# Depthwise convolution of five of eight channel blocks: from scaled additions on VectorE to diagonal products on TensorE

## The chip, the cores and the metric

The kernel runs on one core of one Trainium2 chip. The metric is device time in microseconds, the median of several executions. Engines are named as the profile names them: PE (TensorE; PEld its weight loads), DVE (VectorE), ACT (ScalarE), POOL (GpSimd), SP (SyncE, which here only issues DMAs).

## The reference, cut to what matters

Two layers of a backbone over 256 latent and 256 context tokens with 1024 channels. The change concerns the first layer's mixer: one input projection feeds the heads of a state-space scan (SSD) and a conformer module; both go into one output projection, then a mixture of experts.

```python
def conformer_conv(v, gate, dw_w, dw_b, ln_g, ln_b, rows):
    u = v * jax.nn.sigmoid(gate)
    b, n, ch = u.shape
    if rows is not None:
        u = u.reshape(b * rows, GRID_W, ch)
    u = dwconv(u, dw_w, dw_b).reshape(b, n, ch)
    return jax.nn.silu(layernorm(u, ln_g, ln_b))
```

`dwconv` is a depthwise convolution along the tokens: 31 taps here, a weight for each tap and channel, zeros beyond the ends. The context is one sequence of 256 tokens; the latent tokens are four rows of 64, each convolved by itself.

## The kernel before, in words

Activations lie with 128 channels on the partitions and 512 tokens (256 context, 256 latent) on the columns. A **piece** is one block of 128 output columns of the input projection: 24 products of 128x128 weights with 512 columns (`cm_gemm`), in which weights and activations are split in high and low parts. Each piece needs its weights split first (`prep`, L465 on ACT, L466 on POOL), in one of two buffers. Weights come over SP's queue in 1 MB units into a ring of three tiles (`Stream`), in the order in which the program plans them.

The program is written in one order, and each engine keeps it. Work beside the products is written as generators: `step()` (L131) moves each one a step on, and `bg(us)` does so after a part of a piece and moreover takes entries from the list `bgq`, `RATE[0]` of them per microsecond of products (0.6, later 1.4). So what stands between two products in an engine's queue is set by these steps.

Four stretches follow each other, after a beginning of some 55 us:

- The SSD channels: 16 pieces, each followed by `conv5` (five taps on DVE, L772 and L774, then silu and transposes, L799). `CV_AT` puts three conformer blocks between them; a conformer block (`cvg_task`) is two pieces, value and gate.
- The SSD scan (`states`, `group`, `rest`: 16 groups of four heads) beside the list `FILL`: the two pieces each of the other five conformer blocks, and 16 modulation blocks (`mod_task`), each of two halves of four products with 32 weight columns in four column tiles (weights `sT`, moving columns from the ring).
- Eight pieces z that gate the SSD heads (`z_gate`, L1117 to L1129). What is left in `bgq` is written out behind them.
- The output projection, with the layer norm of the conformer channels beside its first half; then the experts and layer 1.

For each conformer block `cf_evac` writes the gated values into the tile `u`, rows with 15 zeros between them (602 columns), and puts 31 taps into `bgq`. A tap (L702, L704, L706) is one instruction on DVE over 572 columns: it adds `u`, shifted by the tap's place and scaled by that tap's weight of each channel, to one of two sums `ca`. The last one adds the two sums (L709, L710).

Of the kernel before, what the change touches and what calls it, by code (L numbers as in the profile page):

```python
# [27 lines left out]
class Stream:  # L28
    """Weights in the order of use, 2048 values a partition at a time, loaded ahead through rings of tiles."""
# [16 lines left out]
    def ring(self, tiles, last=None):  # L46
        """tiles [128, 2048] for the units up to the one of the key last"""
        self.rings.append((list(tiles), len(self.plan) if last is None else self.index[last] + 1))
        self.fill()

    def hold(self, held, fence=None):
        """no more loads for a while, for what must not wait behind them; fence: done on the next tile before its load"""
        self.held, self.fence = held, fence
        self.fill()

    def until(self, key=None, fence=None):
        """nothing after the unit of the key for now; fence: done on the next tile before its load"""
        self.limit = 1 << 30 if key is None else self.index[key] + 1
        self.fence = fence
        self.fill()  # L60
# [29 lines left out]
def build(tc, I, out):  # L90
# [32 lines left out]
    # ------------------------------------------------------------------ work beside the products  # L123
# [7 lines left out]
    def step(us=0.0, rate=0.0):  # L131
        """one step of everything that goes on beside the products, which took us since the last one"""
# [26 lines left out]
    class Slots:  # L159
        """tiles of rotating buffers, handed out when the last use of the buffer has been written down"""  # L160
# [17 lines left out]
        def take(self, *a):  # L178
            """for the work beside the products"""
            n = 0  # L180
            while (x := self.now(*a)) is None:
                n += 1
                assert n < 500
                yield
            return x

        def main(self, *a):
            """for the products"""
# [14 lines left out]
    # ------------------------------------------------------------------ the order of the weights  # L203
# [32 lines left out]
    CV_AT = {1: 0, 4: 1, 7: 2}  # L236
# [12 lines left out]
    for i in range(3, 8):  # L249
        for q in range(2):  # L250
            FILL.append(("cvg", i, q))
            for _ in range(2 if i < 7 else 0):
                FILL.append(MODS.pop(0))
    for f in FILL:
# [34 lines left out]
    # ------------------------------------------------------------------ constants  # L289
# [17 lines left out]
    def unit(pool, name, dt=F32):  # L307
        """8 KB of each partition; a later one of the same name takes the place of the first"""
# [68 lines left out]
    # 0 and 1 are exact in float32r  # L377
# [6 lines left out]
    # conditioning columns, silu, padded to 32 columns  # L384
# [23 lines left out]
    # ------------------------------------------------------------------ modulation  # L408
# [17 lines left out]
    def mod_block(l, b):  # L426
        """512 columns of the modulation of both conditionings, as columns [128, 4, 2]"""
# [19 lines left out]
    def row_bcast(dst, col):  # L447
        """dst [128, 1024] = the vector whose columns col(c) -> [128, 1], on every partition"""
# [12 lines left out]
    # ------------------------------------------------------------------ hi / lo parts of weights  # L461
    def prep(buf, w, eng=GP):
        """w [128, a, b] of 1024 values a partition -> its float32r high and low parts"""
# [5 lines left out]
    class Pieces:  # L469
        """the pieces of a list, prepared ahead in the free pairs of buffers"""  # L470
# [4 lines left out]
        def buffers(self, units, end=None):  # L475
            """for the pieces before the position end"""
# [13 lines left out]
        def release(self, n=None):  # L490
            """done with the n oldest pieces handed out"""
# [4 lines left out]
        def next(self, keep=False):  # L496
            """the next piece; the ones before it are done with, unless to be kept"""
# [63 lines left out]
    # ------------------------------------------------------------------ layer 0: norm, transposed input  # L561
    def quarter(u, i):
        """512 values of each partition of the tiles u"""
# [21 lines left out]
    def to_channels(p, k, gain, shift, hi, lo):  # L585
        """channel block k of the four token tiles, transposed -> modulated, split"""
# [21 lines left out]
    # the products over the first half of the input channels run before the second half is there  # L608
# [33 lines left out]
    stt.close()  # L642

    # ------------------------------------------------------------------ layer 0: input projection
# [15 lines left out]
    # layout of the padded conv input: 15 | ctx 256 | 15 | row 64 | 15 | row 64 | ... | 15  # L660
# [58 lines left out]

    def cm_task(sink):  # L720
        """one channel block; sink(accumulator) one step later"""
# [28 lines left out]
    def cvg_task(i):  # L750
        cm_task(lambda acc: PA.update(v=acc))
        cm_task(lambda acc: begin(cf_evac(i, PA.pop("v"), acc)))

    # SSD channels
# [59 lines left out]
    def lower_bounds():  # L814
        """of the forget gates: second row of the softmax over the layers"""
# [13 lines left out]
    def step_sizes(acc):  # L829
        """softplus, token-major [128, direction, tile, head]; decays"""  # L830
# [55 lines left out]
    begin(step_sizes(first[0]))  # L886
    for q in range(2):
        begin(conv5(8 + q, first[1 + q]))
    for i in range(8):
        for q in range(2 if i else 0):  # L890
            cm_task(lambda acc, j=2 * i + q: begin(conv5((8 + j) % 16, acc)))
        if i in CV_AT:
            cvg_task(CV_AT[i])
    drain()
    st1.close()

    # ------------------------------------------------------------------ layer 0: SSD beside the rest of the projection
# [17 lines left out]
    # high and low parts of the log decays  # L915
# [13 lines left out]
    def states():  # L929
        """carried states of both directions: decay * the one before + sum over the tile of B x dt decay-to-end"""  # L930
# [46 lines left out]
    def group(t, g):  # L977
        """the part of a tile's own tokens, for the four heads of a group"""
        b = []
        # log decays of the steps, of those up to each column  # L980
# [12 lines left out]
        # log decay from the row to the column, in whichever direction  # L993
# [27 lines left out]
        # channels of four heads on the partitions, tokens on the columns  # L1021
# [15 lines left out]
    def rest(t, hf):  # L1037
        """xs[t][hf] becomes the sum of the skip and state terms; added to the tile's own part"""
# [64 lines left out]
    # ------------------------------------------------------------------ layer 0: gate of the SSD heads  # L1103
# [57 lines left out]
    # ------------------------------------------------------------------ layer 0: output projection, conformer layer norm  # L1161
# [5 lines left out]
    # ------------------------------------------------------------------ router, fed while the output projections end  # L1167
# [12 lines left out]
    # the channels of the conformer, high and low  # L1180
# [6 lines left out]
    def router_pre(l, streams, pool):  # L1187
        """router weights times the gain of the norm, what its shift adds to the scores; both as rows"""
# [23 lines left out]
    def router_pair(X, streams, xg, pr, hf):  # L1212
        """512 columns of two tiles of X: squares of the norm, times the gain, transposed into the scores"""
# [59 lines left out]
    def moe_row(xg, t, i, c):  # L1273
        """a tile of rows for the experts; the columns from c on on ScalarE and GpSimd, those before on VectorE"""
# [20 lines left out]
    def ch_total(pq):  # L1295
        """sums of the four rows of each group, on every partition [128, 512]"""
# [10 lines left out]
    def layer_norm():  # L1307
        """beside the products of the first half of the output projection"""
# [66 lines left out]
    def tm_block(lhs, nt, sink, parts=1):  # L1375
        """512 output columns of nt token tiles; sink(t, accumulator) one step after the last product of each"""
# [62 lines left out]
    # ------------------------------------------------------------------ mixture of experts  # L1439
# [6 lines left out]
    # row of the result, row of the token, less BIG  # L1446
# [1279 lines left out]
```

## Time and profile before

| | |
|---|---|
| Device time, median of three runs | 1615.83 us (1612.98 to 1616.37) |
| Profiled execution, first to last instruction | 1616.7 us |
| PE busy, of the span | 1391.0 us (86%) |
| DVE busy | 1065.9 us (66%) |
| ACT busy | 748.6 us (46%) |
| POOL busy | 647.6 us (40%) |
| Taps (L706), count and busy time | 232, 258.4 us |
| HBM read, written | 321.44 MB, 9.44 MB |

Busy times are of one execution. Matmuls are pipelined, so their single durations overlap; the distance between starts is the better price. A mean duration in a group can hold several shapes. An fp32 product has two records. Idle time of an engine is put down to what ended it last.

### The profile page before, as it was taken

Reading aid. Unit: us, or ns where it says so; the run is one execution under the profiler, and the core shown is the slowest. Engines: PE = TensorE matmul, PEld = TensorE weight load, DVE = VectorE, ACT = ScalarE, POOL = GpSimd, SP = SyncE. Lnnn points to the kernel's source line nnn. Section 1 sums busy time; section 2 is a strip of 40 time slices with the busy share of each in tenths; the row PEclk is TensorE's granted clock in tenths of the full one; section 3 lists DMA queues with packets and bytes.
Section 4 is the critical chain, followed back from the end, with each engine's and each line's share of the span. In section 5 each row is a group of like instructions: output and inputs, shape, how many; then the busy total and the mean of one; then the engine's idle time right before and its main releaser. Section 6 shows DMA issues by size and latency. Waiting matters only on the chain. (4 is left out here: it accounts for less than half of the span.)

```text
span 1616.7 us, 18791 instructions
## 1 busy us (share of the span) xinstructions
PE 1391.0 (86%) x6960; PEld 935.1 (58%) x6960; DVE 1065.9 (66%) x1371; ACT 748.6 (46%) x1252; POOL 647.6 (40%) x400
## 2 busy tenths in 40 slices
PE   5997877787788987699999895899999988999995
PEld 2676654554566665566666573688777765444441
DVE  3789999999997476688888885644554644221223
ACT  3443354544324444477777684644453552212112
POOL 4334377876645274354445654342242232000000
PEclk9999987898998998799999998899999999999998
DMA  9223234556324153799998875522123658999990
GB/s 335 90 69 83 64 130 157 174 170 202 94 64 156 52 208 136 275 317 334 337 335 309 291 253 182 192 87 79 53 79 99 227 199 306 370 393 394 393 395 34
DMA packets 178085, 328.03 MB, mean 203 GB/s; under 512 B 7113, under 2 KB 44241, under 8 KB 177472
## 3 DMA queue, kind: packets, MB, share of 16 engines
q1 hardware_dynamic: 172512, 314.08, 55.8%
q0 software_dynamic: 4208, 8.90, 1.8%
q10 hardware_dynamic: 1264, 3.73, 0.6%
q8 instruction: 60, 0.98, 0.3%
q14 instruction: 41, 0.34, 0.1%
HBM read 321.44 MB, written 9.44 MB: 205 GB/s over the span
## 5 line engine op out<-in xcount | busy, mean ns | idle before, releaser
L466 POOL TENSOR_TENSOR wb<-wring,wb 128x1024 fp32r<-128x1024 f32 x68 | 174.8, 2574 | 266.9 <-ACT wb L465 231.0
L706 DVE SCALAR_TENSOR_TENSOR ca<-u,pcol,ca 128x572 f32<-128x572 f32 x232 | 258.4, 1172 | 0.0
L99 PE MATMUL acc<-hh,wb 128*128 128x512 f32 x640 | 217.8, 418 | 16.3 <-DVE u L688 6.3
L99 PEld LDWEIGHTS acc<-hh,wb 128*128 128x128 f32 x640 | 125.2, 198 | 50.6 <-issue 8.0
L465 ACT ACTIVATE wb<-wring 128x1024 fp32r<-128x1024 f32 x88 | 92.3, 1055 | 92.6 <-PE acc L99 50.2
L99 PE MATMUL acc<-hl,wb 128*128 128x512 f32 x320 | 130.0, 406 | 0.3 <-DVE hl L591 0.2
L99 PE MATMUL acc<-wb,um 128*96 128x512 f32 (+1 forms) x480 | 119.8, 399 | 2.9 <-DVE otmp L1416 2.5
L2687 POOL TENSOR_TENSOR xl<-xl,fg 128x512 f32<-128x512 f32 x1 | 1.3, 1267 | 258.7 <-ACT xl L2686 258.7
L2508 DVE TENSOR_TENSOR sg<-sg,y 64x512 f32<-64x512 f32 x16 | 11.1, 692 | 137.8 <-ACT sg L2507 137.8
L99 PEld LDWEIGHTS acc<-wb,um 128*96 128x96 f32 (+1 forms) x480 | 80.3, 169 | 35.4 <-DVE otmp L1416 3.5
L99 PE MATMUL y<-hu,hu 128*64 128x512 f32 (+2 forms) x296 | 91.1, 524 | 2.9 <-DVE hu L2043 2.7
L99 PE MATMUL acc<-wring,sT 128*32 128x512 f32 x336 | 53.7, 721 | 24.6 <-DVE u L688 13.3
L466 DVE TENSOR_TENSOR wb<-uo,wb 128x1024 fp32r<-128x1024 f32 x34 | 55.5, 1663 | 26.5 <-ACT wb L465 26.3
L99 PEld LDWEIGHTS acc<-hl,wb 128*128 128x128 f32 x320 | 62.4, 195 | 15.9 <-DVE hl L591 1.6
L99 PE MATMUL acc<-um,um 128*96 128x512 f32 (+2 forms) x272 | 66.7, 383 | 1.0 <-POOL um L466 1.0
L466 DVE TENSOR_TENSOR wb<-um,wb 128x1024 fp32r<-128x1024 f32 x30 | 52.9, 1803 | 20.3 <-ACT wb L465 20.3
L99 PE MATMUL acc<-uo,um 128*96 128x512 f32 (+1 forms) x240 | 62.9, 401 | 0.0
L466 POOL TENSOR_TENSOR um<-uo,um 128x1024 fp32r<-128x1024 f32 x19 | 47.3, 2488 | 39.0 <-ACT um L465 38.9
L774 DVE SCALAR_TENSOR_TENSOR xa<-xin,pcol,xa 128x514 f32<-128x514 f32 x64 | 56.5, 883 | 2.3
L466 POOL TENSOR_TENSOR um<-wring,um 128x1024 fp32r<-128x1024 f32 x16 | 40.4, 2525 | 40.5 <-ACT um L465 39.0
L99 PE MATMUL acc<-wb,hxh 128*128 128x512 f32 x160 | 52.7, 411 | 0.0
L99 PE MATMUL acc<-wb,uo 128*128 128x512 f32 x192 | 51.0, 413 | 1.6 <-POOL wb L466 1.6
(646 smaller groups left out, 3413.8 us busy)
## 6 DMA issues: line engine op xcount, KB each, us to landing
wring<-in_mod_w_dram SPq DMA_DIRECT2D x42, 1024.0 KB, 5.2
wring<-in_moe_w_gate_dram SPq DMA_DIRECT2D x18, 1024.0 KB, 7.6
uo<-in_moe_w_up_dram SPq DMA_DIRECT2D x17, 1024.0 KB, 7.6
hu<-in_moe_w_gate_dram SPq DMA_DIRECT2D x16, 1024.0 KB, 14.6
wring<-in_moe_w_down_dram SPq DMA_DIRECT2D x14, 1024.0 KB, 7.5
uo<-in_moe_w_down_dram SPq DMA_DIRECT2D x13, 1024.0 KB, 7.4
um<-in_moe_w_up_dram SPq DMA_DIRECT2D x13, 1024.0 KB, 7.6
wring<-in_hg_w_in_dram SPq DMA_DIRECT2D x13, 1024.0 KB, 5.2
```

What stands on the lines that cost most here:

```text
L99: PE.matmul(o, l, r, start=start, stop=stop, skip_group_check=True)
L465: SC.activation(hv, w, AF.Copy)
L466: eng.tensor_tensor(lv, w, hv.bitcast(F32), op=ALU.subtract)
L706: DV.scalar_tensor_tensor(a, x, w, a, op0=ALU.mult, op1=ALU.add)
L774: DV.scalar_tensor_tensor(a[:, 0:514], x[:, k:k + 514], par("sc_w", 16 * k + i), a[:, 0:514], op0=ALU.mult, op1=ALU.add)
L2508: DV.tensor_tensor(s_[up], s_[up], acc[up], op=ALU.mult)
L2687: GP.tensor_tensor(o, o, fg[hf], op=ALU.mult)
```

## The change

Blocks 0 to 4 of the eight are convolved on PE, blocks 5 to 7 as before. All five are now projected in the first stretch (`CV_AT`), so FILL has three blocks and the same 16 modulation blocks.

For such a block `cf_rows` writes the gated values once, as eight rows of 94 columns (64 values with 15 on each side; the four rows of the context take their edges from their neighbours), sends the tile to DRAM and reads it back four times: group j of 32 partitions gets 32 channels at a time, shifted by j columns. So the 128 partitions hold four taps of 32 channels. `tap_columns` lays out the weights in the same way once, and `cf_rows` makes of them 32 diagonal weight tiles of 128x32 (one operation on DVE). `cf_task`, at the places of `CF_AT`, multiplies: eight steps of four taps, in each of them four groups of 32 channels on four column tiles, 32 fp32 products a block, summed in one accumulator. ACT adds the bias.

```diff
-    CV_AT = {1: 0, 4: 1, 7: 2}
+    NPE = 5
+    CV_AT = {0: 0, 1: 1, 3: 2, 4: 3, 6: 4}
+    CF_AT = {2: (0,), 3: (1,), 5: (2,), 6: (3,), 7: (4,)}
...
     FILL = []
     MODS = [("mod", 0, b) for b in range(4, 12)] + [("mod", 1, b) for b in range(8)]
-    for i in range(3, 8):
+    for i in range(NPE, 8):
         for q in range(2):
             FILL.append(("cvg", i, q))
-            for _ in range(2 if i < 7 else 0):
+            for _ in range(3 if i < 7 else 2):
                 FILL.append(MODS.pop(0))
+    assert not MODS
     for f in FILL:
...
+    stcf = ExitStack()
+    cfp = stcf.enter_context(tc.tile_pool(name="cfp", bufs=1))
...
+    RW, UW, NX = 94, 756, 750
+    u94 = [cfp.tile([128, UW], F32, name=f"u94{i}") for i in range(2)]
+    for u in u94:
+        GP.memset(u, 0.0)
+    U94 = Slots(*((lambda u=u: u, 1) for u in u94))
+    UX = Slots((lambda: cfp.tile([128, 4, NX], F32, name="ux", tag="ux", bufs=2), 2))
+    DG = Slots((lambda: cfp.tile([128, 32, 32], F32, name="dg", tag="dg", bufs=1), 1))
+    uD = dram.tile([NPE, 128, UW], F32, name="uD")
+    wtap = quarter(um, 19)[:, 0:256].rearrange("p (b m g) -> p b m g", b=8, m=8)
+    CX = {}
+
+    def tap_columns():
+
+        GP.memset(wtap, 0.0)
+        p = yield from TRS.take()
+        pv = p.ap[:, 0:256].rearrange("p (b m g) -> p m b g", b=8, m=8)
+        for g in range(4):
+            for j in range(4):
+                n = 8 if j < 3 else 7
+                a = par("cf_w", 8 * j, 8)
+                src = bass.AP(tensor=a.tensor, offset=a.offset, ap=[list(a.ap[0]), [32, n], [1, 8]])
+                mm(pv[32 * j:32 * j + 32, 0:n, :, g], ident[:, 32 * g:32 * g + 32], src, g == 0, g == 3)
+        yield
+        SC.activation(wtap[0:96].rearrange("p b m g -> p (b m g)"), p.ap[0:96, 0:256], AF.Copy)
+        SC.activation(wtap[96:128].rearrange("p b m g -> p b (m g)")[:, :, 0:28],
+                      p.ap[96:128, 0:256].rearrange("p (b x) -> p b x", b=8)[:, :, 0:28], AF.Copy)
+        p.done()
+
+    def cf_rows(i, av, ag):
+
+        sgs = yield from SGS.take()
+        sg = sgs.ap
+        SC.activation(sg, ag.ap, AF.Sigmoid)
+        ag.done()
+        us = yield from U94.take()
+        u = us.ap[:, 0:8 * RW].rearrange("p (r c) -> p r c", c=RW)
+        yield
+        r64 = lambda x: x.rearrange("p (r c) -> p r c", c=64)
+        DV.tensor_tensor(u[:, :, 15:79], r64(av.ap), r64(sg), op=ALU.mult)
+        av.done()
+        sgs.done()
+        SC.activation(u[:, 0:3, 79:94], u[:, 1:4, 15:30], AF.Copy)
+        SC.activation(u[:, 1:4, 0:15], u[:, 0:3, 64:79], AF.Copy)
+        dgs = yield from DG.take()
+        DV.tensor_tensor(dgs.ap, bc(ident4[:, None, :], [128, 32, 32]),
+                         bc(wtap[:, i].rearrange("p m g -> p (m g)")[:, :, None], [128, 32, 32]), op=ALU.mult)
+        yield
+        SY.dma_start(uD[i], us.ap)
+        us.done()
+        yield
+        ux = yield from UX.take()
+        a = uD[i]
+        for j in range(4):
+            SY.dma_start(ux.ap[32 * j:32 * j + 32],
+                         bass.AP(tensor=a.tensor, offset=a.offset + j, ap=[[UW, 32], [32 * UW, 4], [1, NX]]))
+        CX[i] = (ux, dgs)
+
+    def cf_task(i):
+        n = 0
+        while i not in CX:
+            step()
+            n += 1
+            assert n < 500
+        ux, dgs = CX.pop(i)
+        acc = ACC.main()
+        for m in range(8):
+            for g in range(4):
+                a = ux.ap[:, g, 4 * m:4 * m + 64]
+                x = bass.AP(tensor=a.tensor, offset=a.offset, ap=[list(a.ap[0]), [RW, 8], [1, 64]])
+                mm(acc.ap[32 * g:32 * g + 32], dgs.ap[:, 4 * m + g], x, m == 0, m == 7)
+            if m % 4 == 3:
+                bg(3.6)
+        ux.done()
+        dgs.done()
+
+        def sink():
+            o = quarter(um, 12 + i)
+            SC.activation(o, acc.ap, AF.Identity, bias=par("cf_b", i))
+            acc.done()
+            co[i] = o
+        pend.append(sink)
+
     def cm_task(sink):
...
     def cvg_task(i):
         cm_task(lambda acc: PA.update(v=acc))
-        cm_task(lambda acc: begin(cf_evac(i, PA.pop("v"), acc)))
+        cm_task(lambda acc: begin(cf_rows(i, PA.pop("v"), acc)))
...
     begin(step_sizes(first[0]))
+    begin(tap_columns())
     for q in range(2):
...
         if i in CV_AT:
             cvg_task(CV_AT[i])
+        for b in CF_AT.get(i, ()):
+            cf_task(b)
     drain()
+    stcf.close()
     st1.close()
```

The order of DVE's queue in the first stretch, between the second conformer block and the next SSD channels. `xa` are the sums of the five taps of SSD channels, `ca` those of the 31. Before:

```order
L687 TENSOR_TENSOR u<-acc_966,sg 128x256
L688 TENSOR_TENSOR u<-acc_966,sg 128x4x64
L702 TENSOR_SCALAR ca<-u,pcol 128x572
L704 TENSOR_SCALAR ca<-u,pcol 128x572
L772 TENSOR_SCALAR xa<-xin_425,pcol 128x514
L774 SCALAR_TENSOR_TENSOR xa<-xin_425,pcol,xa 128x514 x4
L706 SCALAR_TENSOR_TENSOR ca<-u,pcol,ca 128x572 x3
L772 TENSOR_SCALAR xa<-xin_426,pcol 128x514
L774 SCALAR_TENSOR_TENSOR xa<-xin_426,pcol,xa 128x514 x4
L706 SCALAR_TENSOR_TENSOR ca<-u,pcol,ca 128x572 x4
```

Now (`dg` are the diagonal weights):

```order
L766 TENSOR_TENSOR u_429<-acc_1001,sg 128x8x64
L772 TENSOR_TENSOR dg<-ident_146,um_101 128x1024
L862 TENSOR_SCALAR xa<-xin_434,pcol 128x514
L864 SCALAR_TENSOR_TENSOR xa<-xin_434,pcol,xa 128x514 x4
L862 TENSOR_SCALAR xa<-xin_435,pcol 128x514
L864 SCALAR_TENSOR_TENSOR xa<-xin_435,pcol,xa 128x514 x4
```

No tap stands between the SSD channels any more; the gating and one operation of 1024 columns come once for each block.

DVE's queue in the second stretch, at the first SSD groups (`sc` are masked scores, `modc` a modulation block's result). Before:

```order
L970 TENSOR_TENSOR cb_1488<-acc_1490,mU 128x512
L970 TENSOR_TENSOR cb_1489<-acc_1490,mL 128x512
L706 SCALAR_TENSOR_TENSOR ca<-u,pcol,ca 128x572 x2
L1014 TENSOR_TENSOR sc<-seg,cb_1488 128x512
L706 SCALAR_TENSOR_TENSOR ca<-u,pcol,ca 128x572 x7
L1014 TENSOR_TENSOR sc<-seg,cb_1488 128x512
L423 TENSOR_REDUCE modc_166<-tr 128x8
L424 TENSOR_TENSOR modc_166<-modc_166,pcol 128x8
L706 SCALAR_TENSOR_TENSOR ca<-u,pcol,ca 128x572 x8
```

Now:

```order
L1064 TENSOR_TENSOR cb_1776<-acc_1778,mU 128x512
L1064 TENSOR_TENSOR cb_1777<-acc_1778,mL 128x512
L1108 TENSOR_TENSOR sc<-seg,cb_1776 128x512 x2
L427 TENSOR_REDUCE modc_166<-tr 128x8
L428 TENSOR_TENSOR modc_166<-modc_166,pcol 128x8
```

The taps that are left (66 in this stretch, 142 before; 21 in the z pieces, 42 before) begin after the second piece of block 5.

SP's queue at the end of the first stretch (`wring` are the ring's tiles, `uD` the copy in DRAM, `ux` what is read back). Before:

```order
L76 DMA wring_106<-in_ab_w_in_dram 128x8x256
L76 DMA wring_104<-in_ab_w_in_dram 128x8x128 x2
L76 DMA wring_105<-in_ab_w_in_dram 128x8x128 x2
L76 DMA wring_106<-in_mod_w_dram 128x4x512
L76 DMA wring_104<-in_mod_w_dram 128x4x512
```

Now:

```order
L775 DMA uD<-u_430 128x756
L781 DMA ux<-uD 32x4x750 x4
L76 DMA wring_105<-in_mod_w_dram 128x4x512
L76 DMA wring_106<-in_mod_w_dram 128x4x512
L775 DMA uD<-u_429 128x756
L781 DMA ux<-uD 32x4x750 x4
L76 DMA wring_104<-in_mod_w_dram 128x4x512
```

A block's five transfers stand between the weight loads; the copies wait for the landing of the write.

## Rows read from the trace of the kernel before

**Rows 1.** By stretch: length, PE, PEld, DVE, ACT, POOL busy, clock, DMA, GB/s.

```profile
55.00:207.50 152.50, 128.18 (x549) 101.06 (x547) 143.08 (x168) 60.92 (x151) 55.10 (x24) 0.94 0.24 69
207.50:441.00 233.50, 185.60 (x1066) 118.16 (x1065) 225.94 (x248) 105.58 (x265) 172.31 (x131) 0.88 0.51 160
441.00:507.00 66.00, 54.45 (x206) 42.35 (x205) 63.70 (x79) 20.91 (x28) 34.89 (x14) 0.87 0.29 88
```

**Rows 2.** PE's groups by shape, 207.5 to 441 us: busy, mean ns | idle before, releasers.

```profile
L99 PE MATMUL acc<-wring,sT 128*32 128x512 f32 x256 | 41.6, 730 | 17.9 <-DVE u L688 13.3 <-DVE t L1056 2.5 <-issue 2.1
...
L99 PE MATMUL y<-sc,xd 128*64 128x128 f32 x256 | 21.7, 317 | 16.7 <-DVE modc L423 9.2 <-DVE sc L1014 6.7 <-POOL sc L1014 0.7
```

**Rows 3.** PE's timeline, first stretch: start, length, [idle before, releaser].

```profile
105.62 2.26 PE L99 MATMUL acc<-hh,wb 128*128 128x512 f32 x9
...
111.22 2.26 PE L99 MATMUL acc<-hh,wb 128*128 128x512 f32 x9
...
139.00 0.66 PE L799 MATMUL tr<-ident,sg 128*128 128x128 f32 x4 [2.66 <-ACT sg L783]
139.41 2.34 PE L99 MATMUL acc<-hh,wb 128*128 128x512 f32 x9
...
206.65 1.11 PE L799 MATMUL tr<-ident,sg 128*128 128x128 f32 x4 [4.79 <-ACT sg L783]
```

**Rows 4.** Waits in the first stretch: total, times, longest.

```profile
ACT sg L783 <- DVE xa L774: 42.6, 8, 6.4
```

**Rows 5.** DVE's timeline, first stretch.

```profile
157.73 0.42 DVE L687 TENSOR_TENSOR u<-acc,sg 128x256 f32<-128x256 f32 x1
...
166.50 2.62 DVE L772 TENSOR_SCALAR xa<-xin,pcol 128x514 f32<-128x514 f32 x1
169.16 3.12 DVE L774 SCALAR_TENSOR_TENSOR xa<-xin,pcol,xa 128x514 f32<-128x514 f32 x4
...
177.25 0.54 DVE L772 TENSOR_SCALAR xa<-xin,pcol 128x514 f32<-128x514 f32 x1
177.82 3.12 DVE L774 SCALAR_TENSOR_TENSOR xa<-xin,pcol,xa 128x514 f32<-128x514 f32 x4
...
183.03 2.63 DVE L772 TENSOR_SCALAR xa<-xin,pcol 128x514 f32<-128x514 f32 x1
```

**Rows 6.** PE's timeline, second stretch: halves of modulation blocks.

```profile
241.00 1.07 PE L99 MATMUL acc<-wring,sT 128*32 128x512 f32 x8
242.00 0.50 PE L99 MATMUL tr<-sb0h,mSL 128*128 128x512 f32 x1
...
250.51 1.93 PE L99 MATMUL acc<-wring,sT 128*32 128x512 f32 x8 [5.27 <-DVE u L688]
```

**Rows 7.** DVE's groups, whole span: an operation of 1024 columns.

```profile
L466 DVE TENSOR_TENSOR wb<-uo,wb 128x1024 fp32r<-128x1024 f32 x34 | 55.5, 1663 | 26.5 <-ACT wb L465 26.3
```

**Rows 8.** DMA issues: count, KB each, median us from issue to landing.

```profile
wring<-in_ab_w_in_dram SPq DMA_DIRECT2D x8, 1024.0 KB, 5.4
...
hD<-um SPq DMA_DIRECT2D x4, 512.0 KB, 2.6
```

**Rows 9.** DVE's groups, 207.5 to 441 us: the taps.

```profile
L706 DVE SCALAR_TENSOR_TENSOR ca<-u,pcol,ca 128x572 f32<-128x572 f32 x142 | 163.8, 1209 | 0.0
```

**Rows 10.** POOL's groups, 207.5 to 441 us: the low parts of the pieces' weights.

```profile
L466 POOL TENSOR_TENSOR wb<-wring,wb 128x1024 fp32r<-128x1024 f32 x10 | 27.4, 2759 | 0.0
```

**Rows 11.** ACT's groups, 207.5 to 441 us: one of three kinds of mask scalings.

```profile
L990 ACT ACTIVATE sb0h<-mU,lah 128x128 fp32r<-128x128 f32 x64 | 20.3, 394 | 0.0
```

**Rows 12.** Waits, 441 to 507 us.

```profile
PE acc L99 <- DVE u L688: 5.0, 1, 5.0
```

**Rows 13.** Two lines of POOL, 212 to 445 us: duration in ns, min/median/max.

```profile
L1002 POOL TENSOR_TENSOR xd<-um,sm x32: 607/1117/1125, 219.2 to 417.6; 128x256 f32<-128x256 f32 x32
...
L987 POOL TENSOR_TENSOR sb1h<-mL,lah x16: 1029/1544/1551, 215.6 to 416.0; 128x512 fp32r<-128x512 f32 x16
```

**Rows 14.** Waits, 207.5 to 441 us.

```profile
ACT seg L1007 <- PE tr L99: 50.0, 12, 9.7
...
POOL sc L1014 <- ACT seg L1007: 23.9, 6, 6.0
```

## The prediction

> **What bounds the kernel now.** I read the busy times by stretch first, because an average over the whole span mixes stages [rows 1]. Three stretches hold everything that the change touches. In **A** (55 to 207.5 us, the input projection) DVE is busy for 143.1 of 152.5 us, PE for 128.2. In **B** (207.5 to 441, the SSD work beside the rest of the projection) DVE is busy for 225.9 of 233.5, PE for 185.6, POOL for 172.3. In **C** (441 to 507, the eight z pieces) it is 63.7 of 66.0 against 54.5. So VectorE is full in all three, and PE has holes at a mean granted clock of 0.94, 0.88 and 0.87.
>
> PE's groups by shape tell what the holes hang on [rows 2]. In B, PE waits 13.3 us ahead of modulation products for the gating of the next conformer block, and ahead of the SSD's last products 9.2 us for the small modulation add and 6.7 us for the masked scores. All three are short instructions that stand behind taps in DVE's queue. The timeline of A shows the same: PE sits idle before the transposes, 2.7 us at 139.00 and 4.8 at 206.65 [rows 3], ScalarE waits 42.6 us for the five-tap convolution of the SSD channels [rows 4], and DVE's own timeline repeats with a period of 183.03 - 166.50 = 16.5 us for two channel blocks [rows 5]. PE needs 2 x 5.6 us for the two pieces and 0.4 us for each group of transposes (139.00 to 139.41), 12.0 us. DVE is the bound there, by 4.5 us a pair.
>
> **Stretch A, after.** It gets four more pieces. One piece is 5.60 us, from 105.62 to 111.22 [rows 3]: **+22.4**.
>
> It gets 5 x 32 diagonal products, K = 128, 32 columns of weights, 512 moving columns, fp32, four neighbours on four column tiles. The nearest rows have exactly this shape: the modulation products, whose eight records (two for each fp32 product) take 1.00 us from the start to the next instruction's start at full clock, and 1.9 us where the clock was low [rows 6]. I take 1.0 us a four, because the stretch keeps PE busy: 5 x 8 x 1.0 = **+40**, at most 76. The moving rows are eight runs of 64 with a step of 94; no row here shows that, and I take the price of the contiguous one.
>
> The row behind the modulation products starts with no gap although the tile mode changes. The Trainium skill (TensorEngine Tiling (Array Packing), section Key Properties) says that changing the tiling mode drains TensorE. By that rule the six runs of conv products, twelve changes, would cost an estimated 12 x 0.5 us, the length of the product at 242.00, and the forecast would be 6 us higher; the row shows none of it.
>
> The sixteen small products that lay out the tap columns: between nothing and 4 us (four fours). I take **+2**.
>
> Taken away: the holes. From 139 to 207.5 us the program has 8.3 pieces and seven transposes, 49.6 us of work in 68.5, so 19 us are lost. Without taps, DVE needs for a pair 2.63 + 3.12 + 0.54 + 3.12 = 9.4 us [rows 5], below PE's 12. What the change puts there, a gating of 0.8 us (two halves of 0.42 now) and the diagonal weights, 1.7 us like another 128x1024 operation [rows 7], comes once per block and fits too. I take **-19**, at least -10.
>
> The transfers: one block is written to DRAM (0.39 MB) and read back four times (1.5 MB). A 512 KB write landed in 2.6 us, a 1 MB load in 5.4 [rows 8]: some 2.6 + 8.1 = 10.7 us. Blocks 0 to 3 have four to six pieces (22 to 34 us) of cover. The last has two: the diagonal buffer is single, so its generator goes on only after block 3's products, and its write stands on SP behind two weight loads that wait for POOL. The cover is 11.2 us; without it all 10.7 would show. I take **+1**, bounds 0 to 6. The weight loads behind these waits were issued three tiles ahead, two pieces a tile, 22 us or more before use: nothing, at most 5.
>
> A: 22.4 + 40 + 2 - 19 + 1 = **+46**, 43 to 98.
>
> **Stretch B, after.** It loses four of ten pieces and, by the order, 76 of 142 taps (66 stand in B in the changed program). DVE: 225.9 - 76 x 1.154 (163.8 / 142 [rows 9]) and 6 us for the ends of two blocks, 132 us. POOL: 172.3 less four weight differences of 2.8 us [rows 10], about 160. PE: 185.6 - 22.4 = 163. **TensorE becomes the longest.** Its idle 47.9 us hold 29.2 that PE's rows put down to DVE's gating (13.3), modulation add (9.2) and score products (6.7); those I let go, 19 remain. The new order ends B with two SSD groups that have no piece beside them. A group's chain is some 8 us: twelve mask scalings, 0.39 us each [rows 11], then products, exponential, masking, products. Against that stands a clock that is held better; I let these two cancel. B: 163 + 18 = 181, so **-52**. Bounds: 160 (below) to 211 (below).
>
> **Stretch C, after.** PE needs 8 x 5.6 = 44.8 us; DVE has 21 taps instead of 42 and falls to some 40. Of the 21 us lost, a wait of 5.0 us for the gating [rows 12] among them, I keep 8 because the taps that are left stand in the first pieces: 53, **-13**, bounds -6 to -18. Behind 507 us nothing moves: the layer norm waits for z's end, not for the taps, which end before it.
>
> **Sum.** 46 - 52 - 13 = -19 us against the profiled execution's span of 1616.7 us; the median of the runs, 1615.8, lies 0.9 below it. Forecast: **1597 us**. New work is 42 us on PE (40 + 2). PE is idle now for 24 + 48 + 12 = 84 us of the three stretches [rows 1], besides what a low clock costs it. The change pays if more than 42 us of all that come back.
>
> **Rivals.** (1) *GpSimd speeds up as well.* POOL's instructions spread widely beside the taps: 607 to 1117 ns, 1029 to 1544 ns for one shape [rows 13]. If most return to the short end, a quarter or more of POOL's 160 us goes, no engine but PE is near its limit, and B ends at PE's work at a nearly full clock (163 x 0.92 = 150 us) and a tail of 10: 160 us instead of 181, **1576 us**. Against it: 66 taps and all SSD operations of DVE remain in B. The Trainium skill (SBUF — State Buffer, section Who interferes with whom) says that a VectorE instruction with two SBUF inputs and a GpSimd instruction that reads SBUF exclude each other; the spread of the rows agrees with it. Chance 0.20.
>
> (2) *Slower: the SSD chain itself sets B's pace.* The 16 groups take 14.6 us each; ScalarE waits 50.0 us for PE and POOL 23.9 us for ScalarE [rows 14], a ring that no tap stands in. If that ring and not the taps holds the pace, B loses only its pieces, 233.5 - 22.4 = 211. Then 46 - 22 - 13 = +11: **1627 us**. It decides as soon as B stays above 200 us. Against it: the short DVE members of the ring are themselves queued behind taps. Chance 0.18.
>
> (3) *The diagonal products cost more*: low clock, or strides, or late copies. At 1.93 us a four it is 5 x 8 x 0.93 = 37 us more, **1634 us**. For it: nothing here shows that access or a read of 3000-byte rows at odd offsets; against it, the same shape runs at 1.0 us. Chance 0.09.
>
> (4) *Nothing to see*: gain and new work cancel, **1616 us**. Chance 0.05.
>
> The forecast has 0.48. About 0.2% (3 us) is what a measurement of this kernel can tell from no change. Faster: 0.46 of the forecast, rival 1 and a part of rival 4, 0.68. Within: 0.07. Slower: rivals 2 and 3 except their mild ends: 0.25. The range reaches from rival 1's far side to rival 2's: 1572 to 1630.
>
> **What would show it.** In the profile after: DVE no longer full in A and B (about half busy in A); a conv task of about 8 us on PE, eight fours of 1.0 us, without a wait before it except the last; no waits of PE for the conv chain's transposes; A about 199 us long, B about 181, C about 53. Wrong if: four conv products take much over 1.0 us, PE waits for the copies, or B stays above 200 us with DVE idle.

## The result and the profile after

| | before | after |
|---|---|---|
| Device time, median of four runs | 1615.53 us | 1602.01 us (1599.42 to 1605.88) |
| Ratio to before | | 0.9916, 95% interval 0.9897 to 0.9934 |
| Profiled execution | 1616.7 us | 1599.4 us |
| Taps on DVE | 232, 258.4 us | 87, 110.0 us |

The change makes the kernel faster by 13.5 us (0.8%); the forecast of 1597 was 5 us low. The sum came out, but not by its own terms: in the profiled execution the first and third stretch were shorter than forecast (9 and 7 us), the second 20 us longer.

The same cuts as in [rows 1], of the changed kernel (length, busy time of PE, PEld, DVE, ACT and POOL, granted clock, DMA share, GB/s):

```profile
55.00:245.10 190.10, 182.15 (x1000) 125.88 (x999) 106.45 (x119) 78.36 (x179) 61.76 (x26) 0.98 0.46 118
245.10:445.80 200.70, 159.04 (x979) 101.27 (x977) 135.39 (x165) 98.07 (x258) 141.18 (x125) 0.91 0.53 176
445.80:492.10 46.30, 46.30 (x193) 37.15 (x194) 41.85 (x45) 18.32 (x25) 28.35 (x13) 0.97 0.42 125
```

Forecast were 199, 181 and 53 us. PE is nearly full in A (8 us idle) and full in C. In B it is idle for 41.7 us at a clock of 0.91, although DVE has work for only two thirds of the time.

PE's timeline in A (start, length, records, wait and releaser) shows the new products; they answer to [rows 3] and [rows 6]:

```profile
103.93 2.03 PE L99 MATMUL acc<-hh,wb 128*128 128x512 f32 x8
105.89 7.08 PE L99 MATMUL acc<-ux,dg 128*32 128x512 f32 x64
112.89 0.50 PE L99 MATMUL acc<-hh,wb 128*128 128x512 f32 x1
...
233.82 8.76 PE L99 MATMUL acc<-ux,dg 128*32 128x512 f32 x64 [6.54 <-DMA ux<-uD]
242.51 0.66 PE L889 MATMUL tr<-ident,sg 128*128 128x128 f32 x4
244.57 0.66 PE L889 MATMUL tr<-ident,sg 128*128 128x128 f32 x4 [1.41 <-ACT sg L873]
```

A block takes 7.0 us from its start to the next instruction. That is 0.88 us a four (four neighbouring products on the four column tiles, eight records), with no gap on either side. The waits ahead of the SSD transposes, 2.7 and 4.8 us in [rows 3], are gone but for 1.4 us. The last block is the exception: 6.5 us of waiting for its copies, and products that then run slower, 8.76 us.

What PE waits for in B, by the list of waits (total, times, longest), against [rows 2] and [rows 14]:

```profile
PE y L99 <- DVE sc L1108: 15.6, 5, 4.6
PE y L99 <- POOL um L1152: 6.4, 2, 3.7
PE acc L99 <- DVE S L1051: 5.1, 1, 5.1
...
PE acc L99 <- DVE u L694: 2.6, 1, 2.6
```

23.3 us end with a short DVE operation: the masked scores `sc`, the state `S`, the gating `u`. Of the three kinds that the prediction let go (gating 13.3, modulation add 9.2, scores 6.7, together 29.2 us), 18.2 are left. The gating fell to 2.6 and the modulation add is gone, but the scores rose to 15.6. One wait for the scores, in the timelines of ScalarE, DVE and PE:

```profile
389.13 0.60 ACT L1101 ACTIVATE seg<-tr 128x512 f32<-128x512 f32 x1 [4.89 <-PE tr L99]
```

```profile
378.70 14.49 DVE L712 SCALAR_TENSOR_TENSOR ca<-u,pcol,ca 128x572 f32<-128x572 f32 x8
393.11 0.18 DVE L427 TENSOR_REDUCE modc<-tr 128x8 f32<-128x32 f32 x1
393.32 0.17 DVE L428 TENSOR_TENSOR modc<-modc,pcol 128x8 f32<-128x8 f32 x1
393.41 2.25 DVE L712 SCALAR_TENSOR_TENSOR ca<-u,pcol,ca 128x572 f32<-128x572 f32 x3
395.58 0.68 DVE L1108 TENSOR_TENSOR sc<-seg,cb 128x512 f32<-128x512 f32 x1
```

```profile
337.14 1.09 PE L99 MATMUL y<-sc,xd 128*64 128x128 f32 x16 [2.70 <-DVE sc L1108]
...
389.88 1.92 PE L99 MATMUL acc<-wring,sT 128*32 128x512 f32 x16
396.41 1.98 PE L99 MATMUL y<-sc,xd 128*64 128x128 f32 x16 [4.60 <-DVE sc L1108]
...
410.63 1.09 PE L99 MATMUL y<-sc,xd 128*64 128x128 f32 x16
```

ScalarE ends the exponential that `sc` needs at 389.7 us (389.13 + 0.60). The masking stands behind a run of eight taps and one of three, and begins 6 us later; PE has run out of work at 391.8. The products behind this wait take 1.98 us for 16 records. The same group takes 1.09 us behind no wait (410.63), and also behind the wait of 2.70 us (337.14).

### The profile page after: what moved, and what is told of

Read it like the earlier page. It is cut to its first block, busy times and chain, and to the rows that moved or that the text cites. A ratio compares the mean times of both kernels' runs of the same rounds, so it can differ in the third digit from the quotient of the medians.

```text
span 1599.4 us, 19406 instructions
## 1 busy us (share of the span) xinstructions
PE 1408.0 (88%) x7312; PEld 936.3 (59%) x7312; DVE 916.7 (57%) x1206; ACT 755.7 (47%) x1269; POOL 617.5 (39%) x398
## 5 line engine op out<-in xcount | busy, mean ns | idle before, releaser
L470 POOL TENSOR_TENSOR wb<-wring,wb 128x1024 fp32r<-128x1024 f32 x68 | 169.6, 2498 | 273.6 <-ACT wb L469 231.5
L99 PE MATMUL acc<-hh,wb 128*128 128x512 f32 x640 | 207.4, 401 | 4.5 <-POOL wb L470 2.4
L99 PEld LDWEIGHTS acc<-hh,wb 128*128 128x128 f32 x640 | 119.7, 189 | 38.7 <-issue 5.9
L712 DVE SCALAR_TENSOR_TENSOR ca<-u,pcol,ca 128x572 f32<-128x572 f32 x87 | 110.0, 1321 | 0.0
L470 POOL TENSOR_TENSOR um<-uo,um 128x1024 fp32r<-128x1024 f32 x19 | 47.3, 2487 | 39.2 <-ACT um L469 39.2
L99 PE MATMUL acc<-wring,sT 128*32 128x512 f32 x336 | 47.6, 647 | 11.2 <-DVE xld L582 6.2
L99 PEld LDWEIGHTS acc<-um,um 128*96 128x96 f32 (+1 forms) x272 | 43.5, 174 | 15.5 <-POOL um L470 1.3
```

What stands on the lines that cost most here:

```text
L99: PE.matmul(o, l, r, start=start, stop=stop, skip_group_check=True)
L470: eng.tensor_tensor(lv, w, hv.bitcast(F32), op=ALU.subtract)
L712: DV.scalar_tensor_tensor(a, x, w, a, op0=ALU.mult, op1=ALU.add)
```

## The experiments

All are the changed kernel with one edit, unless said otherwise. To be free of the start, which differs by up to 5 us between executions, the stretches are cut at events of the program: A from the transposes of the step sizes (61.86 us in the changed kernel) to the first instruction behind the last SSD transposes, B from there to the first z piece, C to the first transposes of the output projection, and the rest to the end of the span. The ratio is that to the kernel before in runs on the same chip.

| kernel | A | B | C | rest | median us | ratio (95%) |
|---|---|---|---|---|---|---|
| before | 147.0 | 233.6 | 65.7 | 1110.0 | 1615.5 | 1 |
| after | 183.1 | 200.8 | 46.3 | 1107.3 | 1602.0 | 0.9916 (0.9897 to 0.9934) |
| e_b_notaps | 123.0 | 177.4 | 46.8 | 1105.3 | 1512.2 | 0.9343 (0.9321 to 0.9365) |
| e_notaps | 184.5 | 159.2 | 47.0 | 1100.9 | 1557.0 | 0.9624 (0.9599 to 0.9649) |
| e_rate | 184.5 | 173.5 | 56.2 | 1115.5 | 1594.1 | 0.9842 (0.9820 to 0.9866) |
| e_dg2 | 185.3 | 201.3 | 46.6 | 1107.5 | 1604.2 | 0.9917 (0.9897 to 0.9938) |
| e_hold | 174.8 | 201.3 | 46.3 | 1110.9 | 1599.3 | 0.9885 (0.9859 to 0.9911) |
| e_double | 213.5 | 201.6 | 46.3 | 1104.4 | 1633.9 | 1.0109 (1.0080 to 1.0139) |
| e_pace2 | 184.3 | 185.4 | 50.6 | 1105.8 | 1599.1 | 0.9891 (0.9864 to 0.9917) |
| e_npe3 | 146.4 | 219.2 | 62.8 | 1106.0 | 1602.1 | 0.9928 (0.9913 to 0.9943) |
| e_six14 | 193.8 | 173.6 | 47.3 | 1105.0 | 1584.4 | 0.9801 (0.9775 to 0.9826) |
| e_best6 | 193.8 | 160.3 | 47.5 | 1105.5 | 1572.3 | 0.9725 (0.9699 to 0.9751) |
| e_best6p | 193.8 | 172.9 | 49.1 | 1107.3 | 1588.8 | 0.9843 (0.9826 to 0.9860) |
| e_best7 | 212.4 | 148.2 | 47.1 | 1108.6 | 1577.1 | 0.9764 (0.9750 to 0.9777) |

### What holds B: taps left out

```diff
-                else:
-                    DV.scalar_tensor_tensor(a, x, w, a, op0=ALU.mult, op1=ALU.add)
```

Of the changed kernel:

> The changed kernel with 87 taps on VectorE left out: blocks 5 to 7 keep two of their 31 taps each, so their convolution is not the reference's. It asks what holds the second stretch at 201 us instead of 181. Theory T (the taps that are left still stand in runs of up to eight ahead of short SSD operations; PE's idle time there has 23 us that end with such an operation): the second stretch falls to 175 to 182 us, the third stays at 45 to 46, the whole comes to about 1577 us. Theory R (the ring of scalings, exponential, masking and products of the SSD groups holds the pace, the rival on the slower side): the second stretch stays at 196 us or more, the whole at 1596 or more.

The same edit of the kernel before:

> The kernel before with 232 taps on VectorE left out (each of the eight blocks keeps two of 31, so the convolution is not the reference's). Nothing else is moved: the upper end of what taking taps off VectorE can give. Theory T: the first stretch falls from 152 to 130 us, the second from 234 to 200, the third from 66 to 47: 75 us less, about 1540 us. The change then keeps 14 of these 75, after about 42 of new work on PE and about 20 that the taps left in the second and third stretch still take. Theory R: the second stretch stays at 222 us or more, the whole comes to 1560 or more.

B by its length, busy times and clock, e_notaps and then, for all three stretches, e_b_notaps:

```profile
248.00:406.90 158.90, 145.78 (x977) 92.09 (x975) 58.03 (x92) 98.05 (x258) 122.91 (x125) 0.98 0.67 222
```

```profile
55.00:186.10 131.10, 125.70 (x561) 101.31 (x558) 100.38 (x119) 63.58 (x154) 54.40 (x24) 0.97 0.27 81
186.10:365.10 179.00, 166.73 (x1072) 109.57 (x1072) 66.31 (x106) 107.98 (x267) 137.07 (x132) 1.00 0.65 212
365.10:409.90 44.80, 44.80 (x193) 36.00 (x193) 34.15 (x43) 21.34 (x30) 28.39 (x13) 1.00 0.37 118
```

Theory R is out: without taps B falls to 159 us, and the SSD ring is all still there. Theory T holds in kind but was too small: 42 us come back in B, not 23. PE's idle time falls from 41.7 to 13.1 us. Its busy time for the same products falls from 159.0 to 145.8, at a clock of 0.98 instead of 0.91. So the taps cost PE twice, by waits and by the low clock of what it does between them. The kernel before gains 105 us (1617.6 to 1512.2), where 75 were expected. The edit frees POOL too (busy 141.2 to 122.9 us), so it doesn't tell whether the taps cost by standing in DVE's queue or by slowing GpSimd; e_rate does.

The two kernels take the change apart. In B the kernel before loses 56 us to 142 taps (233.6 - 177.4, 0.40 us each). The changed kernel loses 42 to 73 (200.8 - 159.2, 0.57 each). So half the taps gave back only 15 of these 56 us; the other 18 of B's gain are the four pieces that moved (177.4 - 159.2).

### How the taps stand: the rate

```diff
     begin(tiles_of(3))
-    RATE[0] = 1.4
+    RATE[0] = 0.7
```

> The changed kernel with the rate at which taps are put between the products of the second stretch halved, from 1.4 to 0.7 a microsecond, so that they stand in runs of two to four, not of up to eight; what is left over goes to the third stretch. Theory T: PE's waits for short operations of VectorE fall from 23 to about 12 us, the second stretch to about 190; the third may grow by up to 3; the whole is faster by 8 us (4 to 12). Theory R: no change within 2 us, or slower by what the third stretch grows.

B falls by 27 us, more than expected, with 52 taps in it instead of 73. C, which takes 35 instead of 14, grows by 10, and what follows by 8; 8 us remain by the medians (12 by the ratios, 0.9842 against 0.9916).

B and C by their busy times, then two of PE's waits in B:

```profile
249.60:422.80 173.20, 150.21 (x977) 95.24 (x975) 116.89 (x140) 97.98 (x258) 141.16 (x125) 0.96 0.61 204
422.80:478.90 56.10, 49.14 (x192) 38.45 (x193) 55.14 (x67) 16.61 (x23) 34.48 (x11) 0.93 0.29 86
```

```profile
PE y L99 <- DVE sc L1108: 4.6, 3, 3.2
...
PE acc L99 <- DVE S L1051: 2.1, 1, 2.1
```

With the gating's 2.6 us, PE's waits for short DVE operations fall from 23.3 to 9.3 us. POOL's busy time in B is what it was (141.16 us against 141.18), so the 27 us do not come from a faster GpSimd. In DVE's timeline of B the taps stand in runs of 4.0 on average in the changed kernel, 3.8 in the kernel before and 2.2 here. The edit changes two things at once, the length of the runs and the number of taps in B: at 0.57 us a tap, the 21 fewer would be an estimated 12 of the 27 us. The runs do not separate the two further.

DVE is full in C again (55.14 of 56.10 us). With 87 taps on DVE neither of the two rates suits both stretches.

### The last block's copies

```diff
-    DG = Slots((... bufs=1), 1))
+    DG = Slots((... bufs=1), 1), (lambda: um[4][:, 512:1536]..., 1))
```

> The changed kernel with a second buffer for the diagonal weights (in space that is free in this stretch), so that the last block's rows are written to DRAM before the products of the block ahead of it, and its copies have more than two pieces of cover. Theory D (the single buffer makes the last block's copies late): the wait of 6.5 us ahead of the last conv products goes, and with it the low clock of those products, 1.7 us: first stretch 190 to about 183, the whole faster by 6 us (4 to 8). Rival: the copies wait in SP's queue behind weight loads, and no more than 3 us come back.

No change: the wait is 7.55 us. SP's timeline in the changed kernel tells why (start, length):

```profile
199.12 18.09 SPq L76 DMA_DIRECT2D wring<-in_mod_w_dram  x2
217.30 0.46 SPq L775 DMA_DIRECT2D uD<-u  x1
224.39 1.75 SPq L781 DMA_DIRECT2D ux<-uD  x4
```

The second weight load waits for its tile until 217 us, and the write behind it waits too, though its rows are ready at 213.4 (the last edge copy ends there on ACT). Then the write takes until 224.4 to land, beside the 1 MB load issued just ahead of it. With a second buffer this was the same, 3 us later in that execution (220.26 and 228.12).

```diff
+            if CV_AT[i] == NPE - 1:
+                S.hold(True)
             cvg_task(CV_AT[i])
...
+        if i == NPE - 1:
+            S.hold(False)
         dgs = yield from DG.take()
```

The `dg` part stands behind the transfers here.

> The changed kernel with the last block's five transfers put ahead of two weight loads in SP's queue (the loads are held back until the transfers are issued), and each block's transfers written down ahead of its diagonal weights. The second buffer for the diagonal weights changed nothing: the last write was issued right behind a weight load that stood on SP for 18 us until its tile came free. Theory Q (SP's order makes the copies late): the write is issued some 6 us earlier, the wait of 6.5 us ahead of the last conv products shrinks to 0 to 2, those products run at the full clock (7.1 us instead of 8.8), the first stretch is 7 us shorter, the whole faster by 7 us (4 to 9) than the changed kernel. Rival: write and read back take their 16 us from wherever they start and the held loads are late for the first modulation products; no more than 2 us come back.

SP's timeline and then PE's (this execution begins 3.2 us later):

```profile
216.56 0.34 SPq L772 DMA_DIRECT2D uD<-u  x1
219.06 1.75 SPq L778 DMA_DIRECT2D ux<-uD  x4
```

```profile
228.40 2.03 PE L99 MATMUL acc<-hh,wb 128*128 128x512 f32 x8
230.36 7.07 PE L99 MATMUL acc<-ux,dg 128*32 128x512 f32 x64
```

The wait is gone and the products run at full clock: A is 8 us shorter. The write was issued 4 us earlier, not 6, and landed in 2.4 us instead of 7, with no load ahead of it. Over the runs this is some 5 us (0.9885 against 0.9916); the intervals overlap, so the whole's gain is likely, not shown.

### The products doubled

```diff
-                mm(acc.ap[32 * g:32 * g + 32], dgs.ap[:, 4 * m + g], x, m == 0, m == 7)
+                mm(acc.ap[32 * g:32 * g + 32], dgs.ap[:, 4 * m + g], x, m == 0, False)
+                mm(acc.ap[32 * g:32 * g + 32], dgs.ap[:, 4 * m + g], x, False, m == 7)
```

> The changed kernel with every diagonal product of the five blocks made twice into the same accumulator (the five blocks' convolution comes out doubled). It prices the products in place. If the first stretch is bound by PE, it grows by the products' own length, 5 x 7.1 = 35 us, and the whole comes to about 1637 us. If something else sets the pace there, the growth is under 20 us.

```profile
193.67 14.02 PE L99 MATMUL acc<-ux,dg 128*32 128x512 f32 x128
...
259.87 15.69 PE L99 MATMUL acc<-ux,dg 128*32 128x512 f32 x128 [2.12 <-DVE xa L865]
```

A grows by 30.4 us. A block goes from 7.08 to 14.02, 6.94 more, 34.7 for five; the wait ahead of the last block's products falls from 6.5 to 2.1 us, which together gives 30.3. That the longer products cover the copies is likely, not shown: the trace puts the 2.1 us down to `xa` on DVE. So A is bound by PE, and a run of conv products has a fixed part of 0.14 us (7.08 - 6.94) at most.

### The groups' pace

```diff
-    begin(tiles_of(3))
+    begin(tiles_of(2))
```

> The changed kernel with an SSD group begun every two steps instead of every three. The changed kernel has fewer pieces in the second stretch, so fewer steps, and its last 20 us hold two groups with no piece beside them; PE is idle for 10 of these. Theory S (the groups run out of products to stand beside): they end with the list of products, the second stretch is 4 to 8 us shorter. Rival: the groups are held by their buffers or wait behind taps, as before; no change within 2 us, or slower.

Inconclusive. The profiled execution is 11 us shorter than that of the changed kernel, B 15; but the six runs spread from 1590.7 to 1604.0, and their ratio (0.9891) is not apart from the changed kernel's. In this execution, the fastest of the six, PE waits only 0.2 us for the scores on DVE, although the taps stand in runs as long as before (4.0 on average). So the length of the runs alone does not set that wait.

### How many blocks

Three blocks (`CV_AT = {1: 0, 3: 1, 5: 2}`, `CF_AT = {3: (0,), 5: (1,), 7: (2,)}`, two modulation blocks behind a piece, as before):

> Three blocks on TensorE instead of five: the first stretch projects three blocks, as in the kernel before, the list of the second has five blocks and 16 modulation blocks, as before; only the taps of these three blocks go. By the price of taps from the two kernels without taps (0.38 us for each of the 142 before in the second stretch): first stretch 147 - 24 + 3 x 7.1 = 144 to 148 us counted from the step-size transposes; second 234 less 39 taps, 214 to 222; third unchanged at 62 to 66: the whole faster than the kernel before by 12 to 22 us, that is as fast as with five blocks or faster. If moving the pieces out of the second stretch is itself what pays, three blocks give less than 8 us.

All three stretches come as expected, and three blocks are as fast as five. The two further blocks cost A 36.7 us and give back 18.4 in B and 16.5 in C. At a rate of 1.4 they pay nothing.

Six blocks, with e_hold's order, the rate of 0.7 and four modulation blocks behind each of the four pieces left:

```diff
-    NPE = 5
-    CV_AT = {0: 0, 1: 1, 3: 2, 4: 3, 6: 4}
-    CF_AT = {2: (0,), 3: (1,), 5: (2,), 6: (3,), 7: (4,)}
+    NPE = 6
+    CV_AT = {0: 0, 1: 1, 2: 2, 4: 3, 5: 4, 6: 5}
+    CF_AT = {2: (0,), 3: (1,), 4: (2,), 5: (3,), 6: (4,), 7: (5,)}
```

> Six blocks on TensorE instead of five, taps put at 0.7 a microsecond in the second stretch instead of 1.4, and the last block's transfers ahead of the held weight loads. Theory T: first stretch 190 + 11.2 + 7.1 - 7 = 201 us; second: two pieces less and some 40 taps in runs of two to four, 150 to 158; third 46 to 49: the whole faster than the changed kernel by 20 to 30 us, about 1577. If the SSD groups' own chain limits the second stretch once the taps are few (16 groups, 10 us each), it stays at 165 or more and the whole at 1587 or more.

```profile
257.30:417.40 160.10, 138.05 (x929) 86.03 (x928) 101.84 (x129) 92.73 (x253) 129.98 (x122) 0.96 0.63 214
417.40:464.90 47.50, 47.45 (x192) 38.01 (x193) 43.04 (x47) 18.62 (x26) 29.16 (x13) 0.94 0.39 122
```

1572 us, 2.8% faster than the kernel before and the fastest of those run: B falls by 40 us (to 160, where 150 to 158 was expected), and C, still full on PE, takes the 16 taps that are left over (47.5 us, against 46.3). Which part of it paid was asked with the old rate (1.4) in the same kernel:

> The six-block kernel with the old rate of taps in the second stretch, 1.4 a microsecond. It separates the sixth block from the rate. If the rate is what paid, the 29 taps fewer give what the changed kernel shows for a tap in that stretch (42 us for 73 taps, 0.57 each: 16 us) and two pieces less 11 us: second stretch 201 - 27 = 174 us, and the whole about 1586. If the sixth block alone did it, the second stretch is 160 to 163 as at 0.7, and the whole within 3 us of 1572.

B is 173.6 us where 174 was expected, the whole 1584. So of the 30 us between e_best6 and the changed kernel some 12 are the rate (43 taps in B instead of 53, and shorter runs); the rest is e_hold's order and the sixth block together.

Seven blocks, with the other edits of e_best6 (eight modulation blocks behind each of the two pieces left):

> As the six-block kernel, with seven blocks on TensorE: the first stretch grows by two pieces and a block of products, 18 us; the second loses two pieces (11 us) and 29 taps. Counted on PE's work alone it is 7 us more; if the 43 taps left in the second stretch still cost 0.3 us each, it is even, 1569 to 1576. If with two pieces left the SSD groups have too little beside them (16 groups in 145 us), the second stretch stays above 150 us and the whole is slower than six blocks by 8 us or more.

1577 us, near the even case (1569 to 1576): B loses 12 us, A gains 18.6. Of the kernels run, six blocks are fastest, by 5 us in the medians; the two intervals just touch. Six blocks with e_pace2's edit:

> The six-block kernel with an SSD group begun every two steps instead of three. With five blocks this took 11 us off the profiled second stretch, but the median of the runs moved by only 4, so it is open. If groups begun earlier use the products that stand there, the second stretch falls from 160 to about 152 and the whole by 4 to 10 us; if POOL's scalings and ScalarE's then come late, no change within 3 us.

Slower by some 19 us than e_best6 (0.9843 against 0.9725): B grows by 13 us at a clock of 0.91, which neither case of the expectation had. PE hardly waits for the scores there (0.3 us). Its waits end with the state `S` on DVE (6.4 us), with ring loads (6.0) and with ScalarE (10.4). Why stays open.

## Why the prediction was right, and where not

**A: right in kind, 9 us too long**, and outside its own bounds (+43 to +98; A grew by 37.6 us by the cuts of [rows 1], by 36.1 by those at events). Pieces: 22.4, as forecast. Products: 40 forecast, 35.4 measured (five times 7.08), because fours that follow each other cost 0.88 us and the price of 1.0 was that of single halves. Holes: -19 forecast, -24 by e_b_notaps (147.0 to 123.0). Tap columns: 2 forecast, 0.65 measured, at 59.32 us and so ahead of the cut at events. Copies: **this term failed**, +1 with an upper bound of 6, measured 6.5 and another 1.7 for the slow products behind the wait. The text counted 10.7 us for the way through DRAM by landings in an idle queue; from issue to the first product it was 16.5, and e_hold names the two parts that had no price, the queue ahead of the write, which the text mentions, and the load beside it, which it does not. The terms without the tap columns sum to 42.0, A grew by 36.1. Some 4 us of the gap are other waits of PE, which e_b_notaps has and the changed kernel hasn't (idle 5.4 us there; 8.0 here, with the copies' 6.5); the rest is not placed.

On the change of tiling mode the row decided rightly. By the rule of the Trainium skill (TensorEngine Tiling (Array Packing), section Key Properties) that changing the tiling mode drains TensorE, the forecast would have been 6 us higher, an estimated 1.0 us for each run; e_double leaves 0.14.

**B: the step that failed.** "Its idle 47.9 us hold 29.2 that PE's rows put down to DVE's gating (13.3), modulation add (9.2) and score products (6.7); those I let go, 19 remain." They did not go: 18.2 of the 29.2 us are still there, 15.6 of them for the scores, and with the state's 5.1 us the waits for short DVE operations are 23.3. Idle time in B was 41.7 us, where the sum has 18. These waits hang on the taps that stand in front of a short operation, as e_notaps shows, and the program sets how densely these stand by `RATE[0]`, which the change leaves at 1.4: fewer taps begin later and stand as densely (runs of 4.0, 3.8 before). Halving the rate took the 23.3 us to 9.3. The sum treated a wait as if it went with the taps that leave. It also had 66 taps in B, by the program's order; 73 ran there. PE's own work was right (163 forecast, 159 measured). The tail without pieces was foreseen, and cancelled against "a clock that is held better"; the tail is there, the clock rose only from 0.88 to 0.91, and e_notaps puts that down to the taps that are left (0.98 without them).

**C: right in kind, 7 us too long.** 53 forecast, 46.3 measured, past the bound of -18; the taps that are left end with the fourth piece, and PE never waits. **The rest**: 2.7 us shorter, forecast nothing; the kernels here differ by more.

**The rivals.** Rival 1's premise came true and its effect did not. POOL's times in B moved to the short end (medians 1117 to 632 ns and 1544 to 1153), against [rows 13]:

```profile
L1096 POOL TENSOR_TENSOR xd<-um,sm x32: 607/632/1127, 252.9 to 433.1; 128x256 f32<-128x256 f32 x32
...
L1081 POOL TENSOR_TENSOR sb1h<-mL,lah x16: 1033/1153/1552, 250.8 to 431.6; 128x512 fp32r<-128x512 f32 x16
```

POOL's work fell from 172 to 141 us, but B did not end at PE's work. Waits of PE that end with POOL are 14.6 of its 41.7 idle us, and e_rate takes 27 us off B with POOL's work unchanged. Rival 2's mark, B above 200, was met (200.7), by another mechanism than its own: e_notaps clears the SSD ring. Rival 3 fell with 0.88 us a four.

So 1597 was near because A (9 us), C (7) and the rest (3) were too pessimistic by as much as B (20) was too optimistic. That these errors cancel is luck.

## What to carry to other kernels

When part of a load is taken off an engine, a wait behind the rest of it need not shrink with it: here the wait for the scores rose from 6.7 to 15.6 us. Look at how many long instructions stand in a row in front of the short one that others wait for, and at what sets that number. Here the rate at which they were interleaved was worth nearly as much (12 us at six blocks) as the whole change (13.5), by shorter runs and by fewer taps in that stretch together. And a transfer on a queue with waiting loads costs what stands ahead of it and beside it, not its landing time in an idle queue.

## What the runs showed of the hardware

- A matmul's moving rows as eight runs of 64 with a step of 94 cost no more than contiguous ones: 0.88 us for a four, where single halves of modulation blocks took 1.00 ([rows 6]).
- A tap took 0.74 us in one run (six in 4.43) and 1.81 us in another (eight in 14.49); in the first case POOL was idle, in the second it was busy for all of 376 to 388 us. The rule of the Trainium skill (SBUF — State Buffer, section Who interferes with whom) agrees: a VectorE instruction with two SBUF inputs contends with a GpSimd instruction that reads SBUF.

```profile
421.39 4.43 DVE L712 SCALAR_TENSOR_TENSOR ca<-u,pcol,ca 128x572 f32<-128x572 f32 x6
```

- Around the run of eight PE's clock fell from full to 0.76 (mean of 12 us), so part of the stretch behind the wait ran at 1.2 GHz. Of the 42 us that 73 taps cost in B, 13 are longer busy time of PE for the same products:

```profile
376.00:388.00 12.00, 9.05 (x59) 6.20 (x58) 11.96 (x9) 4.25 (x14) 12.00 (x8) 1.00 0.43 151
388.00:400.00 12.00, 7.40 (x44) 4.51 (x44) 11.96 (x14) 4.58 (x14) 7.49 (x6) 0.76 0.78 274
```

- A write of 378 KB to DRAM landed in 2.4 us with no load ahead of it (e_hold) and in some 7 behind a 1 MB load on the same queue (after).
